# One layer's memory projection moved from the middle of the program to its start, its result kept in DRAM

## The chip, the cores and the metric

The kernel runs on 1 core of one Trainium2 chip. The metric is the device time of one execution in microseconds (us). Engines are named as in the profile: PE is the matmul engine (PEld its weight load), DVE the vector engine, ACT the scalar engine, POOL GpSimd, and SP the engine whose queue issues the DMA transfers.

## What is computed

Two networks run one after the other on x (512 positions x 1024 channels, float32). `first_block` modulates a normalised x by a vector computed from c, projects it, and joins a gated convolution and a four-head recurrence; an FFN follows. `second_block` has two layers with different attentions; each layer also attends to a memory of 256 rows. Cut to what matters here:

```python
# first_block
mod = silu(c) @ w_ada + b_ada                       # 1024 -> 6*1024
sh1, sc1, g1, sh2, sc2, g2 = split(mod, 6)
h = rms_norm(x, norm_mix_g) * (1 + sc1) + sh1
proj = h @ w_in + b_in                              # glu, qk, v, o, gates, merge ...
# second_block
mem_n = rmsnorm(mem, g_mem)                         # mem: 256 x 1024
for i in range(2):
    h = rmsnorm(x, g_mix[i])
    mix, q_mem = mixer(h)                           # i = 0: indexed, i = 1: windowed
    k, v = split(mem_n @ w_mem_kv[i], 2)            # the memory projection, 1024 -> 2*256
    x = x + concat(mix, attend(q_mem, k, v)) @ w_out
    x = x + conv_glu_ffn(rmsnorm(x, g_ffn[i]), ...)
```

The memory projection of layer 1 depends on `mem`, `g_mem` and a weight only, not on x.

## The kernel before

Activations lie with channels on the partitions: eight tiles of 128x512. For float32 accuracy each operand is split into a rounded high part and a remainder, and each product is three matmuls (`mm3`, L370, L371 and L372 in the profile). Weights are streamed by `unit`: a DMA into `st` (L346 to L348), a cast to `wh` on ACT (L349), the remainder `wl` on DVE or POOL (L352). `st`, `wh` and `wl` have four buffers each, so the transfer into the fifth waits until the first has been read. Activations use slots: 24 of "hs", 22 of "big", 12 of "q", 8 of "t". A Tile scheduler fixes each engine's instruction order when the program is built; on the chip every engine then works strictly in that order, and all DMAs are issued by SP in one order.

The start: `setup` loads c, the eight tiles of x, a vector table and constants. `block1` squares and sums x (L448 on ACT, L452 on DVE), sums over channels and broadcasts the reciprocal root (L465, L473, L475, L491, L494), then for each k of eight channel tiles computes two columns of the modulation (`ada`: four transfers of 256 KB, each reduced by DVE at L602), the gain (L609), the modulated norm (`mod_norm`: L625 on DVE, high part L628 on ACT, remainder L629 on DVE) and 18 matmuls (six output tiles, three each) with `w_glu0`. These 144 matmuls are called the first stage here.

The memory projection (`mem_proj`) takes for each k one unit of weights (128x512) and one tile of the memory (128x256, `memT`), squares the tile (L448), splits it with the gain (L364, L365) and runs 12 matmuls of 128x256; after eight k it copies four sums (L1338), forms the reciprocal root, scales (L1345, L1352) and splits keys and values. For layer 1 it stands at the end of `ffn2(0)`, between that layer's last matmuls and `layer_b`; its tail runs inside `layer_b` (`mid1`):

```python
            self.mem_next = self.mem_proj(1)     # ffn2(0), L1246
            self.some(self.mem_next, 8)
...
        def mid1():                              # layer_b, L1731
            hold["bb"] = self.bcast(hold["rc"])
            self.run_all(self.mem_next)
```

Of the kernel before, what the change touches and what calls it, by code (L numbers as in the profile page):

```python
# [4 lines left out]
F32 = mybir.dt.float32  # L5
# [3 lines left out]
ALU = mybir.AluOpType  # L9
# [3 lines left out]
P = 128  # L13
S = 512
D = 1024
KD = D // P
# [6 lines left out]
MEM = 256  # L23
# [76 lines left out]
def _pairs(a, b):  # L100
# [4 lines left out]


_VEC = [
    ("b_ada", 48), ("norm_mix_g", 8), ("b_glu", 16), ("dw_w", 248), ("dw_b", 8),
    ("ln_g", 8), ("ln_b", 8), ("b_pw", 8), ("qkc_w", 64), ("qkc_b", 16), ("b_qk", 16),
    ("b_o", 8), ("b_merge", 16), ("b_if", 1), ("mnorm_g", 8), ("nffn_g", 8), ("fin_g", 8),  # L110
    ("g_mix", 16), ("g_ffn", 16), ("g_mem", 8), ("kv_norm", 2), ("fc_w", 132), ("fc_b", 44),
]
_OFF = {}
_n = 0
# [3 lines left out]
NVEC = _n  # L118
NFIRST = _OFF["b_glu"]
# [107 lines left out]
class Net:  # L227
# [279 lines left out]
    def setup(self):  # L507
        nc = self.nc
        cp = self.cp
        ones = cp.tile([P, P], F32, name="ones")  # L510
        nc.vector.memset(ones, 1.0)
        self.ones = ones
        eps = cp.tile([P, 1], F32, name="eps")
        nc.vector.memset(eps, EPS)
        self.eps = eps
        self.siluc = []
        for i in range(2):
            c = self.t()[0:1, :]
            nc.sync.dma_start(out=c, in_=self.io["c"][:, i * 512:(i + 1) * 512])
            nc.scalar.activation(out=c, in_=c, func=AF.Silu)  # L520
            pt = self.ps()
            nc.tensor.matmul(pt, ones[0:1, :], c, start=True, stop=True)
            self.siluc.append(self.slot("q"))
            nc.scalar.copy(self.siluc[i], pt)

        nc.scalar.activation(out=self.sm(1, "sd")[0:1, :], in_=c[:, 0:1], func=AF.Sqrt, scale=0.0,
                             bias=eps[0:1, :])
        self.x = []
        for k in range(KD):
            x = cp.tile([P, S], F32, name=f"x{k}")  # L530
            self.x.append(x)
            nc.sync.dma_start(out=x, in_=self.io["xT"][k * P:(k + 1) * P, :])
        vec = cp.tile([P, NVEC], F32, name="vec")
        nc.sync.dma_start(out=vec[:, :NFIRST], in_=self.io["vec"][:, :NFIRST])
        self.vec = vec
        cst = cp.tile([P, NCONST], F32, name="cst")
        nc.sync.dma_start(out=cst[:, :P], in_=self.io["const"][:, :P])
        self.cst = cst
        self.ident = cst[:, 0:P]
        self.band = cst[:, P:3 * P]  # L540
        self.inv = {32: cst[:, 3 * P:3 * P + 16], 16: cst[:, 3 * P + 16:3 * P + 24]}
        zeros = cp.tile([P, 2], F32, name="zeros")
        nc.vector.memset(zeros, 0.0)
        self.zeros = zeros
        self.mod = cp.tile([P, 48], F32, name="mod")
        self.aff = cp.tile([P, 16], F32, name="aff")

    def setup_rest(self):
        nc = self.nc
# [660 lines left out]
    def ffn2(self, l):  # L1210
        nc = self.nc
        hold = {}
        h = self.scaled(lambda k: self.v("g_ffn", 8 * l + k))
        acc = self.sumsq(self.x)

        def mid0():
            hold["rc"] = self.rstd(self.colsum(acc), NB, D)

        def mid1():
            hold["bb"] = self.bcast(hold["rc"])  # L1220

        def up(t, pt, act):
            i = t // 2
            if t % 2 == 0:
                a, y = self.t(), self.t()
                nc.vector.tensor_mul(a, pt, hold["bb"])
                w0 = (l * KF + i) * 3
                for step in self.dwconv(y, a, lambda j: self.v("fc_w", w0 + j),
                                        self.v("fc_b", l * KF + i), 3):
                    step()  # L1230
                nc.scalar.activation(out=y, in_=y, func=AF.Silu)
                hold["a"] = y
                return
            b = self.t()
            nc.vector.tensor_mul(b, pt, hold["bb"])  # L1235
            nc.gpsimd.tensor_tensor(out=b, in0=b, in1=hold["a"], op=ALU.mult)  # L1236
            act.append(self.two("big"))
            self.split(act[-1][0], act[-1][1], b)

        def add(n, pt):  # L1240
            nc.vector.tensor_add(self.x[n], pt, self.x[n])

        if l == 0:
            self.groups("f_up0", h, up, lambda f0, n, act: self.tmat("f_down0", f0, n, KD, act, add),
                        (mid0, mid1))
            self.mem_next = self.mem_proj(1)  # L1246
            self.some(self.mem_next, 8)
            return
        ys = []
        ss = [self.sm(2, f"fss{b}", bufs=1) for b in range(NB)]  # L1250
        gf = [self.slot("q"), self.slot("q")]
        for c in range(2):
            nc.sync.dma_start(out=gf[c], in_=self.io["g_fin"][:, c * 512:(c + 1) * 512])

        def turn():
            mid1()
            for b in range(NB):
                for c in range(2):
                    pt = self.ps()
                    for i in range(4):  # L1260
                        self.transpose(pt[:, i * P:(i + 1) * P],
                                       self.x[4 * c + i][:, b * P:(b + 1) * P])
                    ys.append(self.slot("q"))
                    nc.scalar.copy(ys[-1], pt)

        def down(f0, n, act):
            last = f0 + n == KF
            for c in range(2):
                def done(b, pt):
                    y = ys[2 * b + c]  # L1270
                    nc.vector.tensor_add(y, pt, y)
                    if not last:
                        return
                    sq = self.t()
                    nc.scalar.activation(out=sq, in_=y, func=AF.Square, accum_out=ss[b][:, c:c + 1])
                    nc.vector.tensor_mul(y, y, gf[c])
                    if c == 1:
                        t = self.sm(1, "fs1")
                        nc.vector.tensor_add(t, ss[b][:, 0:1], ss[b][:, 1:2])
                        r = self.rstd(t, 1, D, tag="rfin")  # L1280
                        nc.scalar.activation(out=ys[2 * b], in_=ys[2 * b], func=AF.Copy, scale=r)
                        nc.vector.tensor_scalar(out=y, in0=y, scalar1=r, scalar2=None, op0=ALU.mult)
                        for i in range(2):
                            nc.sync.dma_start(
                                out=self.out[0, b * P:(b + 1) * P, i * 512:(i + 1) * 512],
                                in_=ys[2 * b + i])
                self.mmat("f_down1", f0 + c * n // 2, n, act, done, tail=2 if last and c else 0)
        self.groups("f_up1", h, up, down, (mid0, turn))
# [18 lines left out]
        nc.vector.tensor_sub(x[:, :, 0, :], t[0][:, :, 0, :], t[1][:, :, 1, :])  # L1307
        nc.vector.tensor_add(x[:, :, 1, :], t[0][:, :, 1, :], t[1][:, :, 0, :])

    def mem_proj(self, layer):  # L1310

        nc = self.nc
        acc = self.t(MEM)
# [2 lines left out]
        for u in range(KD // 2):  # L1316
            for i in range(2):
                wh, wl = self.unit("w_mem", layer * 4 + u, i)
                k = 2 * u + i
# [4 lines left out]
                hi, lo = both[:, 0:MEM], both[:, MEM:2 * MEM]  # L1324
# [7 lines left out]
                    self.mm3(pv[b], hi[:, r], lo[:, r], wh[:, c], wl[:, c], k == 0, k == KD - 1)  # L1332
                if k < KD - 1:
                    yield
        kv = [self.t(), self.t()]
        kv = [z[:, i * MEM:(i + 1) * MEM] for z in kv for i in range(2)]
        for z, pt in zip(kv, pts):
            nc.scalar.copy(z, pt)  # L1338
        yield
        rc = self.rstd(self.colsum(acc, nb=2), 2, D, tag="rmem")  # L1340
        bc = self.bcast(rc, 2, out=self.t(MEM))
        keys, vals = [], []
        for n in range(2):
            t = self.t(MEM)
            nc.vector.tensor_mul(t, kv[n], bc)  # L1345
            both = self.slot("big", dt=F32R)
            hi, lo = both[:, 0:MEM], both[:, MEM:2 * MEM]
            self.split(hi, lo, t)
            keys.append((hi, lo))
        for b in range(2):  # L1350
            t = self.t(MEM)
            nc.vector.tensor_scalar(out=t, in0=kv[2 + b], scalar1=rc[:, b:b + 1], scalar2=None,  # L1352
                                    op0=ALU.mult)
            vals.append(self.padded(t.rearrange("p (h d) -> p h d", h=4)))
        self.mem = keys, vals

    def padded(self, src, scale=None):

# [360 lines left out]
    def layer_b(self):  # L1719
        nc = self.nc  # L1720
# [9 lines left out]

        def mid1():  # L1731
            hold["bb"] = self.bcast(hold["rc"])
            self.run_all(self.mem_next)

        def done_kv(b, pt):
            rc = hold["rc"][:, b:b + 1]
# [118 lines left out]
    def run(self):  # L1855
        tc = self.tc
        with (tc.tile_pool(name="const", bufs=1) as self.cp,
              tc.tile_pool(name="small", bufs=4) as self.smp,
              tc.tile_pool(name="weights", bufs=3) as self.wp,
              tc.tile_pool(name="slots", bufs=1) as self.sp,  # L1860
              tc.tile_pool(name="psum", bufs=8, space=PSUM) as self.psp):
            self.setup()
            self.block1()
# [24 lines left out]
```

## Time and profile before

| what | value |
|---|---|
| median of 3 runs | 2208.05 us (2207.01 to 2211.64) |
| the profiled execution's own time | 2214.43 us |
| its span (first to last instruction) | 2212.4 us |
| PE busy | 2151.1 us, 97% of the span |
| DVE, ACT, POOL busy | 1470.8, 1036.3, 670.3 us |
| data moved | 217.03 MB, mean 98 GB/s |

Busy time is summed over the whole span; the profiled execution lies 6.4 us above the median, and times inside the program below are those of that one execution. "Granted clock" is the TensorE clock as a share of full speed.

### The profile page before, as it was taken

To read this page: it belongs to the slowest core of one execution; us is meant where nothing else is said; L and a number is where in the kernel's file an instruction comes from. 1 tells how busy PE (TensorE), PEld (TensorE's weight loads), DVE (VectorE), ACT (ScalarE), POOL (GpSimd) and SP (SyncE) were. 2 spreads that over 40 slices of the span, in tenths; PEclk is the share of its full clock that TensorE was granted. 3 is DMA by queue.
4 is the path that set the end of the run, shared out by engine and by line. 5 is a ranking of instruction groups with operands and counts; after the bars stand their busy time and mean duration, and the time that the engine had idled before them with its cause. 6 is when DMAs were issued, how large, how long until landed. Compare 5 with 4: busy or idle time off the path is not lost.

```text
span 2212.4 us, 30653 instructions
## 1 busy us (share of the span) xinstructions
PE 2151.1 (97%) x10708; PEld 1774.0 (80%) x10708; DVE 1470.8 (66%) x2801; ACT 1036.3 (47%) x1953; POOL 670.3 (30%) x606
## 2 busy tenths in 40 slices
PE   6999999999999999998999999999999999999998
PEld 4887778888888989877788888888887878888886
DVE  8889889454876959859975644535546665445354
ACT  3655466654533434644464433423546545324233
POOL 3554454562223626333442110101223321101010
PEclk9999999999999999999999999999999999999999
DMA  7344443233353332321212322332321012223322
GB/s 262 110 135 134 133 133 99 85 96 112 106 163 103 103 102 85 100 72 44 76 48 67 99 92 95 96 96 92 114 90 53 28 54 86 93 94 95 96 94 87
DMA packets 120542, 217.03 MB, mean 98 GB/s; under 512 B 13762, under 2 KB 18114, under 8 KB 120388
## 3 DMA queue, kind: packets, MB, share of 16 engines
q1 hardware_dynamic: 120388, 215.08, 30.7%
q8 instruction: 84, 1.38, 0.2%
q14 instruction: 70, 0.57, 0.1%
HBM read 212.93 MB, written 2.10 MB: 97 GB/s over the span
## 4 chain that ended last, share of the span: by engine, by line
PE 77%; DVE 5%; issue 1%; ACT 1%; POOL 1%; DMA 0%; SPq 0%; ACTq 0%; POOLq 0%; DVEq 0%
PE ps L370 25%; PE ps L371 25%; PE ps L372 25%; PE ps L504 2%; DVE bias L1634 1%; DVE m L1633 1%; DVE bias L1596 0%; DVE x L1510 0%; DVE rope L1305 0%; PE ps L465 0%; DMA q<-in_ada_dram 0%; POOL q L1096 0%; PE ps L494 0%; DVE pt L362 0%; POOL wl L1096 0%
## 5 line engine op out<-in xcount | busy, mean ns | idle before, releaser
L349 ACT CAST wh<-st 128x512 fp32r<-128x512 f32 (+1 forms) x634 | 388.0, 616 | 689.9 <-PE ps L371 429.8
L371 PE MATMUL ps<-hs,wh 128*128 128x512 f32 (+1 forms) x1736 | 662.0, 381 | 4.1 <-DVE hs L629 3.9
L370 PE MATMUL ps<-hs,wh 128*128 128x512 f32 (+1 forms) x1736 | 658.8, 383 | 7.0 <-ACT hs L1001 2.5
L372 PE MATMUL ps<-hs,wl 128*128 128x512 f32 (+1 forms) x1736 | 659.7, 381 | 1.7 <-POOL wl L1096 1.7
L352 DVE TENSOR_TENSOR wl<-st,wh 128x512 fp32r<-128x512 f32 x424 | 307.9, 728 | 206.5 <-ACT wh L349 204.6
L352 POOL TENSOR_TENSOR wl<-st,wh 128x512 fp32r<-128x512 f32 (+1 forms) x210 | 287.5, 1376 | 352.0 <-ACT wh L349 328.8
L370 PEld LDWEIGHTS ps<-hs,wh 128*128 128x128 f32 x1736 | 327.0, 189 | 79.8 <-ACT hs L628 4.7
L371 PEld LDWEIGHTS ps<-hs,wh 128*128 128x128 f32 x1736 | 327.7, 189 | 73.9 <-DVE hs L629 6.5
L372 PEld LDWEIGHTS ps<-hs,wl 128*128 128x128 f32 x1736 | 327.4, 189 | 70.4 <-POOL wl L1096 2.1
L1236 POOL TENSOR_TENSOR t<-t,t 128x512 f32<-128x512 f32 x44 | 69.0, 1569 | 603.0 <-DVE t L1235 533.9
L644 DVE SCALAR_TENSOR_TENSOR big<-ps,vec,big 128x511 f32<-128x511 f32 (+28 forms) x240 | 164.7, 718 | 3.5 <-ACT big L641 3.5
L372 PE MATMUL ps<-big,wl 128*128 128x512 f32 x400 | 156.3, 394 | 2.8 <-DVE wl L352 2.8
L371 PE MATMUL ps<-big,wh 128*128 128x512 f32 x400 | 156.9, 394 | 0.0
L370 PE MATMUL ps<-big,wh 128*128 128x512 f32 x400 | 156.3, 394 | 0.0
L370 PE MATMUL ps<-wh,hs 128*128 128x512 f32 (+1 forms) x320 | 124.3, 394 | 2.9 <-ACT t L952 2.9
L362 DVE TENSOR_TENSOR big<-t,big 128x512 fp32r<-128x512 f32 (+1 forms) x102 | 72.6, 728 | 80.9 <-ACT big L361 80.5
L371 PE MATMUL ps<-wl,hs 128*128 128x512 f32 (+1 forms) x320 | 125.0, 391 | 0.0
L372 PE MATMUL ps<-wh,hs 128*128 128x512 f32 (+1 forms) x320 | 124.6, 389 | 0.0
L452 POOL TENSOR_TENSOR t<-t,t 128x512 f32<-128x512 f32 (+1 forms) x51 | 65.5, 1285 | 173.3 <-ACT t L448 171.6
L361 ACT CAST big<-t 128x512 fp32r<-128x512 f32 (+1 forms) x102 | 52.9, 535 | 105.3 <-POOL t L1236 83.6
L372 PEld LDWEIGHTS ps<-big,wl 128*128 128x128 f32 x400 | 75.1, 188 | 21.2 <-DVE wl L352 3.7
L370 PEld LDWEIGHTS ps<-big,wh 128*128 128x128 f32 x400 | 75.1, 188 | 17.7
(396 smaller groups left out, 3769.8 us busy)
## 6 DMA issues: line engine op xcount, KB each, us to landing
st<-in_f_up_dram SPq DMA_DIRECT2D x176, 256.0 KB, 2.6
st<-in_f_down_dram SPq DMA_DIRECT2D x88, 256.0 KB, 2.6
st<-in_w_up_dram SPq DMA_DIRECT2D x56, 256.0 KB, 2.7
st<-in_ada_dram SPq DMA_DIRECT2D x48, 256.0 KB, 2.7
st<-in_w_down_dram SPq DMA_DIRECT2D x44, 256.0 KB, 2.6
big<-in_ada_dram SPq DMA_DIRECT2D x32, 256.0 KB, 5.1
st<-in_w_qk_dram SPq DMA_DIRECT2D x32, 256.0 KB, 2.7
st<-in_w_ogm_dram SPq DMA_DIRECT2D x32, 256.0 KB, 2.6
```

The costliest lines, as they stand in the source:

```text
L349: nc.scalar.copy(wh, st)
L352: eng.tensor_tensor(out=wl, in0=st, in1=wh.bitcast(F32), op=ALU.subtract)
L361: nc.scalar.copy(hi, src)
L362: nc.vector.tensor_sub(lo, src, hi.bitcast(F32))
L370: nc.tensor.matmul(out, lh, rh, start=start, stop=False)
L371: nc.tensor.matmul(out, lh, rl, start=False, stop=False)
L372: nc.tensor.matmul(out, ll, rh, start=False, stop=stop)
L452: (add or nc.gpsimd).tensor_tensor(out=acc, in0=acc, in1=sq, op=ALU.add)
L504: self.nc.tensor.transpose(out, in_, self.ident[:p, :p])
L644: nc.vector.scalar_tensor_tensor(out=out[:, d:], in0=x[:, :S - d], scalar=w(j), in1=out[:, d:], op0=ALU.mult, op1=ALU.add)
L1236: nc.gpsimd.tensor_tensor(out=b, in0=b, in1=hold["a"], op=ALU.mult)
L1633: nc.vector.max(m8, sc)
```

## The change

The projection of layer 1 is built in `setup`, before x is loaded. `mem_proj` is cut into `mem_sums` (up to the scaled sums) and `mem_split` (the split). `mem_keep` runs `mem_sums(1)` and writes the two result tiles (128x512 each) to a DRAM tile `kept`; `mem_load` reads them back in `layer_b` and splits them. `g_mem` moves into the part of the vector table that is loaded first, this load comes first, and the weight remainders go to POOL from here on (`pool_lo`).

```diff
@@ _VEC
-    ("b_ada", 48), ("norm_mix_g", 8), ("b_glu", 16), ...
+    ("b_ada", 48), ("norm_mix_g", 8), ("g_mem", 8), ("b_glu", 16), ...
@@ setup
+        vec = cp.tile([P, NVEC], F32, name="vec")
+        nc.sync.dma_start(out=vec[:, :NFIRST], in_=self.io["vec"][:, :NFIRST])
+        self.vec = vec
         self.siluc = []
...
-        self.x = []
-        for k in range(KD):
-            x = cp.tile([P, S], F32, name=f"x{k}")
-            self.x.append(x)
-            nc.sync.dma_start(out=x, in_=self.io["xT"][k * P:(k + 1) * P, :])
-        vec = cp.tile([P, NVEC], F32, name="vec")
-        nc.sync.dma_start(out=vec[:, :NFIRST], in_=self.io["vec"][:, :NFIRST])
-        self.vec = vec
...
+        self.pool_lo = 1
+        mem = self.mem_keep()
+        self.some(mem, 4)
+        self.x = []
+        for k in range(KD):
+            x = cp.tile([P, S], F32, name=f"x{k}")
+            self.x.append(x)
+            nc.sync.dma_start(out=x, in_=self.io["xT"][k * P:(k + 1) * P, :])
+        self.run_all(mem)
@@ ffn2
-            self.mem_next = self.mem_proj(1)
-            self.some(self.mem_next, 8)
             return
@@ mem_sums (the end of what was mem_proj)
-        kv = [self.t(), self.t()]
-        kv = [z[:, i * MEM:(i + 1) * MEM] for z in kv for i in range(2)]
+        two = [self.t(), self.t()]
+        kv = [z[:, i * MEM:(i + 1) * MEM] for z in two for i in range(2)]
...
+    def mem_keep(self):
+        _, two = yield from self.mem_sums(1)
+        self.kept = self.dp.tile([P, 2 * S], F32, name="kept")
+        for i in range(2):
+            self.nc.sync.dma_start(out=self.kept[:, i * S:(i + 1) * S], in_=two[i])
+
+    def mem_load(self):
+        two = [self.t(), self.t()]
+        for i in range(2):
+            self.nc.sync.dma_start(out=two[i], in_=self.kept[:, i * S:(i + 1) * S])
+        self.mem_split([z[:, i * MEM:(i + 1) * MEM] for z in two for i in range(2)])
@@ layer_b
         def mid1():
             hold["bb"] = self.bcast(hold["rc"])
-            self.run_all(self.mem_next)
+            self.mem_load()
```

Lines move with the change: what was L602, L625, L628, L629 of `block1` is L607, L630, L633, L634 in the rows of the changed kernel.

The scheduler's order at the start, first on SP, which issues the transfers. Before, these are the rows where the loads of x end and those of the modulation (`in_ada_dram`) begin:

```order
L532 DMA x_102<-in_xT_dram 128x512
L532 DMA x_104<-in_xT_dram 128x512
L534 DMA vec<-in_vec_dram 128x56
L537 DMA cst<-in_const_dram 128x128
L600 DMA big_156<-in_ada_dram 128x512
L600 DMA big_160<-in_ada_dram 128x512
```

With the change, SP's rows 59 to 68 at the end of all 32 modulation loads; `memT` k=4 to k=7 are the tiles q_229, q_255, q_281 and q_307:

```order
L605 DMA big_761<-in_ada_dram 128x512
L605 DMA big_765<-in_ada_dram 128x512
L561 DMA posi<-in_pos_dram 128x4
L1747 DMA sk_15823<-in_sinks_dram 128x16
L348 DMA st_469<-in_w_glu_dram 128x384
L1324 DMA q_229<-in_memT_dram 128x256
L1324 DMA q_255<-in_memT_dram 128x256
L348 DMA st_484<-in_w_glu_dram 128x384
L1324 DMA q_281<-in_memT_dram 128x256
L1324 DMA q_307<-in_memT_dram 128x256
```

Half of the memory's tiles stand behind the last modulation load, and the last two also behind the load into st_484, whose buffer is that of the last `w_mem` unit.

On DVE, before, the start of the program after the memsets (L452 sums the squares of x, L602 reduces a modulation load):

```order
L452 TENSOR_TENSOR t_114<-t_114,t_131 128x512
L602 ISA big_156,ada_158<-big_156,q_79,vec 128x512
L602 ISA ada_158 128x1
L452 TENSOR_TENSOR t_114<-t_114,t_134 128x512
L602 ISA big_160,mod<-big_160,q_86,ada_158 128x512
```

With the change, DVE's rows 79 to 90 (the 32nd modulation load is big_765; L365 is the remainder of a memory tile; rmem is the memory's reciprocal root; t_353 is the sum of the squares of x):

```order
L607 ISA big_765,mod<-big_765,q_90,ada_763 128x512
L607 ISA mod 128x1
L614 SCALAR_TENSOR_TENSOR aff<-mod,vec 128x1
L365 SCALAR_TENSOR_TENSOR q_234<-q_229,vec,q_234 128x256
L365 SCALAR_TENSOR_TENSOR q_260<-q_255,vec,q_260 128x256
L365 SCALAR_TENSOR_TENSOR q_286<-q_281,vec,q_286 128x256
L365 SCALAR_TENSOR_TENSOR q_312<-q_307,vec,q_312 128x256
L475 RECIPROCAL rmem_338<-sd_336 128x2
L491 TENSOR_TENSOR t_342<-cst,rmem_338 128x256
L1348 TENSOR_SCALAR t_328<-t_328,rmem_338 128x256 x2
L1346 TENSOR_TENSOR t_327<-t_327,t_340 128x256 x2
L452 TENSOR_TENSOR t_353<-t_353,t_355 128x512
```

The seven additions for x, which stood ahead of the reductions, now stand behind all 32 of them and behind the memory projection's end; behind them follow eight L630 in a row, then the L634. ACT's order has the squares of x behind the copy of the memory's broadcast in the same way. On PE all 96 matmuls of the projection stand ahead of x's column sums and of the whole first stage.

On PE between the two layers, before (ps_15507 is the last sum of the FFN, q_15547 a memory tile; 96 rows of 128x256 begin here):

```order
L371 MATMUL ps_15507<-big_15298,wh_15515 128x512
L372 MATMUL ps_15507<-big_15297,wl_15516 128x512
L370 MATMUL ps_15534<-q_15547,wh_15539 128x256
L371 MATMUL ps_15534<-q_15547,wh_15539 128x256
L372 MATMUL ps_15534<-q_15547,wl_15540 128x256
```

With the change, the same place (ps_15742 is the last sum of the FFN, hs_15768 the first tile of the next layer's input):

```order
L371 MATMUL ps_15742<-big_15533,wh_15750 128x512
L372 MATMUL ps_15742<-big_15532,wl_15751 128x512
L370 MATMUL ps_15825<-wh_15830,hs_15768 128x512
L371 MATMUL ps_15825<-wl_15831,hs_15768 128x512
```

The 96 matmuls are gone from here. The two reads of `kept` stand in SP's order right behind the column sums of layer 1's input, and their first use on DVE about 60 matmuls later.

## Rows read from the trace of the kernel before

**Rows 1.** The page's busy time of each engine.
```profile
PE 2151.1 (97%) x10708; PEld 1774.0 (80%) x10708; DVE 1470.8 (66%) x2801; ACT 1036.3 (47%) x1953; POOL 670.3 (30%) x606
```

**Rows 2.** Busy times by stretch; the last three columns: granted clock, DMA share, GB/s.
```profile
0.00:10.00 10.00, 3.77 (x4) 1.16 (x4) 2.70 (x7) 8.24 (x14) 0.70 (x6) 1.00 0.70 240
10.00:35.00 25.00, 16.39 (x52) 11.18 (x52) 24.59 (x50) 7.41 (x15) 9.64 (x8) 1.00 1.04 379
35.00:40.00 5.00, 4.46 (x13) 3.51 (x14) 5.00 (x15) 0.72 (x1) 0.00 (x0) 0.66 0.92 314
0.00:61.00 61.00, 42.65 (x141) 29.23 (x142) 49.00 (x102) 23.64 (x42) 21.16 (x23) 0.97 0.72 250
150.00:350.00 200.00, 191.61 (x869) 155.21 (x869) 186.27 (x364) 102.83 (x166) 98.90 (x78) 0.98 0.42 131
```

**Rows 3.** Timeline of ACT at the start: start, duration, instruction, count, idle time before.
```profile
8.90 2.40 ACT L448 ACTIVATE t<-x 128x512 f32<-128x512 f32 x4
14.16 1.02 ACT L349 CAST wh<-st 128x384 fp32r<-128x384 f32 x2 [2.86 <-DMA st<-in_w_glu_dram]
15.18 0.26 ACT L473 ACTIVATE sd<-ps,eps 128x4 f32<-128x4 f32 x1
```

**Rows 4.** The memory tiles' transfers, from issue to landing.
```profile
DMA to landing us min/median/max: 2.0/2.5/3.8
```

**Rows 5.** Timeline of ACT around the projection of layer 1.
```profile
1554.89 0.49 ACT L364 ACTIVATE q<-q,vec 128x256 fp32r<-128x256 f32 x1
...
1595.65 0.92 ACT L1338 COPY t<-ps 128x256 f32<-128x256 f32 x3
...
1621.96 0.37 ACT L499 COPY t<-ps 128x256 f32<-128x256 f32 x1 [0.20 <-PE ps L494]
```

**Rows 6.** Timeline of PE around the projection of layer 1.
```profile
1584.85 0.28 PE L370 MATMUL ps<-q,wh 128*128 128x256 f32 x1
...
1596.36 0.40 PE L370 MATMUL ps<-wh,hs 128*128 128x512 f32 x1
...
1619.43 0.55 PE L465 MATMUL ps<-ones,t 128*128 128x64 f32 x4
...
1620.35 0.39 PE L372 MATMUL ps<-wh,hs 128*128 128x512 f32 x1
...
1621.52 0.58 PE L370 MATMUL ps<-wh,hs 128*128 128x512 f32 x1
```

**Rows 7.** Timeline of DVE at the start.
```profile
9.56 2.28 DVE L452 TENSOR_TENSOR t<-t,t 128x512 f32<-128x512 f32 x3 [0.31 <-ACT t L448]
...
46.52 1.50 DVE L602 CUSTOM_DVE_ANT_0 big<-big,q,ada 128x512 f32<-128x512 f32 x1
...
48.02 0.74 DVE L602 CUSTOM_DVE_ANT_0 big<-big,q,vec 128x512 f32<-128x512 f32 x1
...
53.59 0.74 DVE L625 SCALAR_TENSOR_TENSOR t<-x,aff,ps 128x512 f32<-128x512 f32 x1
54.25 0.31 DVE L609 SCALAR_TENSOR_TENSOR aff<-mod,vec 128x1 f32<-128x1 f32 x1
```

**Rows 8.** Timeline of PE in the first stage, and the next stage's first matmul.
```profile
13.17 1.97 PE L465 MATMUL ps<-ones,t 128*128 128x64 f32 x8 [6.60 <-DVE t L452]
17.73 2.08 PE L494 MATMUL ps<-t,ones 128*128 128x512 f32 x2 [2.59 <-DVE t L491]
...
38.50 0.63 PE L372 MATMUL ps<-hs,wl 128*128 128x512 f32 x1
...
42.27 0.40 PE L371 MATMUL ps<-hs,wh 128*128 128x512 f32 x1
...
44.37 0.39 PE L372 MATMUL ps<-hs,wl 128*128 128x512 f32 x1
...
60.83 0.39 PE L370 MATMUL ps<-hs,wh 128*128 128x512 f32 x1
```

**Rows 9.** Timeline of POOL in the first stage.
```profile
42.21 5.25 POOL L352 TENSOR_TENSOR wl<-st,wh 128x384 fp32r<-128x384 f32 x4 [7.28 <-ACT wh L349]
```

More of the change, by code (lines that the diff above doesn't have):

```diff
@@ L107 @@
 _VEC = [
-    ("b_ada", 48), ("norm_mix_g", 8), ("b_glu", 16), ("dw_w", 248), ("dw_b", 8),
+    ("b_ada", 48), ("norm_mix_g", 8), ("g_mem", 8), ("b_glu", 16), ("dw_w", 248), ("dw_b", 8),
     ("ln_g", 8), ("ln_b", 8), ("b_pw", 8), ("qkc_w", 64), ("qkc_b", 16), ("b_qk", 16),
     ("b_o", 8), ("b_merge", 16), ("b_if", 1), ("mnorm_g", 8), ("nffn_g", 8), ("fin_g", 8),
-    ("g_mix", 16), ("g_ffn", 16), ("g_mem", 8), ("kv_norm", 2), ("fc_w", 132), ("fc_b", 44),
+    ("g_mix", 16), ("g_ffn", 16), ("kv_norm", 2), ("fc_w", 132), ("fc_b", 44),
 ]
@@ L1308, in do_rope, with mem_sums @@
         nc.vector.tensor_add(x[:, :, 1, :], t[0][:, :, 1, :], t[1][:, :, 0, :])
-    def mem_proj(self, layer):
+    def mem_sums(self, layer):
         nc = self.nc
@@ L1341, in mem_proj, with mem_split @@
         bc = self.bcast(rc, 2, out=self.t(MEM))
+        for n in range(2):
+            nc.vector.tensor_mul(kv[n], kv[n], bc)
+        for b in range(2):
+            nc.vector.tensor_scalar(out=kv[2 + b], in0=kv[2 + b], scalar1=rc[:, b:b + 1],
+                                    scalar2=None, op0=ALU.mult)
+        return kv, two
+    def mem_split(self, kv):
         keys, vals = [], []
         for n in range(2):
-            t = self.t(MEM)
-            nc.vector.tensor_mul(t, kv[n], bc)
             both = self.slot("big", dt=F32R)
             hi, lo = both[:, 0:MEM], both[:, MEM:2 * MEM]
-            self.split(hi, lo, t)
+            self.split(hi, lo, kv[n])
             keys.append((hi, lo))
         for b in range(2):
[L1351 to L1354, printed above, removed]
+            vals.append(self.padded(kv[2 + b].rearrange("p (h d) -> p h d", h=4)))
         self.mem = keys, vals
+    def mem_proj(self, layer):
+        kv, _ = yield from self.mem_sums(layer)
+        self.mem_split(kv)
+    def mem_keep(self):
[8 more added lines that the diff above has]
+        self.mem_split([z[:, i * MEM:(i + 1) * MEM] for z in two for i in range(2)])
     def padded(self, src, scale=None):
@@ L1860, in run @@
               tc.tile_pool(name="slots", bufs=1) as self.sp,
+              tc.tile_pool(name="kept", bufs=1, space=bass.MemoryType.DRAM) as self.dp,
               tc.tile_pool(name="psum", bufs=8, space=PSUM) as self.psp):
```

## The prediction

> **What bounds the kernel now.** The page's busy times come first [rows 1]: PE is busy 97% of the span, so inside the program a microsecond of matmuls taken away or a microsecond of PE idleness added is a microsecond of time, unless PE would have waited there anyway. Then the table of stretches, to see where PE does wait [rows 2]: in the first 61 us it is busy 42.65 us and idle 18.35, the largest gap; from 150 to 350 us it waits 200 - 191.61 = 8.4 us. What fills the gap at the start? The DMA share in the same rows: 1.04 of the engines at 379 GB/s between 10 and 35 us, with DVE busy 24.59 of those 25 us. So PE idles at the start because data arrives at a limit and DVE works them off at nearly the same pace. A projection moved there does not meet an idle machine; it meets an idle PE behind a full DMA queue and a full DVE. What counts is therefore the order in which SP, DVE, ACT and PE take the work at the start, since none of them overtakes. The timelines of the start [rows 3, 7, 8] and of the old place [rows 5, 6] give the durations.
>
> **What the change removes.** In the old place PE runs the 96 matmuls from 1584.85 to 1596.36 without a gap: 11.51 us [rows 6]. The tail in layer 1 goes too: the two column sums' four matmuls, 0.55, and from the end of a matmul (1620.35 plus its slot of 0.23) to 1621.52 the broadcast with its wait, 0.94. Together **-13.0 us**, on PE, which is full there. Nothing should take their place: the first input tiles of layer 1 are ready, and the one finished last is first used 84 matmuls later (84 x 0.233 = 19.6 us; the spacing is worked out below). The two reads of `kept` are 256 KB each, land some 2.5 us after issue like the memory's tiles [rows 4], and are used about 60 matmuls (14 us) later. I cost them at nothing; without that cover they would cost up to 2.5 us. The two writes stand behind loads that are needed much later: nothing.
>
> **What it does to the start, step by step.**
> 1. *The transfers.* Up to the last modulation half, SP's new order has 60 transfers: 8 units of `w_mem` (2.10 MB), x (2.10), four memory tiles (0.52), 32 modulation halves (8.39), two `w_glu0` units (0.39), vector table, constants and c (0.58): 14.08 MB. Before, the first 10 us moved 10 x 0.240 = 2.40 MB, then 379 GB/s [rows 2]. So the last half is there at 10 + 11.68/0.379 = 40.8 us. How long after its arrival by rate is data used? Before, 3.44 MB stand up to the first `w_glu0` unit, 12.8 us by rate, and its cast started at 14.16 [rows 3]: 1.4 us. DVE has the last half at 42.2 and is done at about 43.
> 2. *The last two memory tiles.* They stand behind the load into st_484, which waits until POOL has read the last `w_mem` unit. That unit's cast needs the buffer that the k=3 matmuls read, and the k=3 memory tile is the 54th transfer, some 4 us before the last half. Its square, split, matmuls, the cast and POOL's remainder take till about 44. From there issue to landing 2.5 [rows 4] and two issues: the last tile is usable at **47.5**.
> 3. *The projection's end.* ACT's square and high part 2 x 0.49 [rows 5] = 0.9; DVE's remainder 0.4 (half the width of a 0.74 [rows 7]); the last 12 matmuls at 11.51/96 = 0.12 each, 1.4; four copies at 0.31, 1.2; a cast that stands behind them on ACT, 0.5 [rows 3]; then from the column sums to the end of the broadcast's copy, 1619.43 to 1621.96 + 0.37 [rows 5, 6], 2.9. The copy ends at **54.8**.
> 4. *The squares of x* stand behind that copy on ACT: 0.60 each [rows 3], and the seven additions at 0.76 on DVE [rows 7]. First addition after two squares, 1.2; then 5.3: **61.3**. Before, this was over at 13.1, since x came first and the additions stood ahead of the reductions.
> 5. *Root and broadcast:* 1.97 + 0.26 + 0.74 + 2.08 [rows 3, 7, 8] and 0.3 for the reciprocal and hand-overs, an estimate: 5.4. **66.7**.
> 6. *Norm:* eight L630 stand in a row ahead of the first remainder. Two neighbours start 0.66 apart (53.59, 54.25 [rows 7]), so 8 x 0.67 + 0.74 = 6.1: **72.8**. Until then PE can run only six of the stage's 144 matmuls.
> 7. *The stage:* 138 matmuls. Nine lie between 42.27 and 44.37 [rows 8]: 0.233 each, 32.2 us. After idling PE ran slower for a while: from 35 to 40 us the granted clock was 0.66, between the full 2.4 GHz and the lower level of 1.2, and a matmul took 0.63 instead of 0.40 [rows 2, 8]. Some nine such matmuls at 0.2 more: 1.8. Later weights keep up: two casts and two remainders of 1.3 on POOL [rows 9] per 18 matmuls (4.2 us). End at **106.8**.
>
> Before, the next stage began at 60.83 [rows 8]. The start is therefore 46.0 us later. From there PE is almost always busy, so I pass the shift on in full.
>
> **Sum:** +46.0 - 13.0 = **+33.0 us**. Against the profiled execution's own 2214.43 that is 2247.4; it lies 6.4 above the median, and the same difference on the median 2208.05 gives **2241 us**.
>
> **A rule weighed against the trace.** While POOL computes remainders (42.21 to 47.46 [rows 9]), a reduction on DVE that otherwise takes 0.74 takes 1.50 [rows 7]. In the changed order four remainders of `w_mem` and three additions on POOL fall among the reductions. If each stretches one, that is 7 x 0.76 = 5.3 us, and the k=3 remainder on which step 2 rests stands among those reductions. I count nothing, since DVE has waits for data to give in this stretch, and keep 5.3 for the upper end. The Trainium skill, "SBUF — State Buffer", section "Who interferes with whom", says that a DVE instruction with two SBUF inputs contends with a GpSimd instruction that reads SBUF; the trace agrees with 1.50 against 0.74. By that rule, taken to the full, the sum would be 2246 rather than 2241.
>
> **Rivals.**
> - *The projection is hidden in PE's 18.35 idle us* [rows 2], and all that is left is the gain: 2208 - 13 = 2195, faster. For it: 11.5 us of matmuls fit into 18.35 by size. Against it: x's column sums stand behind all 96 matmuls on PE, and their squares behind the memory's tail on ACT. It decides at the place of the squares of x: were the sum of x finished before about 20 us, when the modulation needs it, this would hold. Chance 0.06, for an order on the chip that differs from the one I read.
> - *Only the transfers count:* 3.15 MB more at the start (`w_mem`, memory, early parts) at 379 GB/s is 8.3 us, less 13.0: 2203, a gain of about 0.2%. It needs x's norm to be done early as well, only paced by the later modulation. Chance 0.04, about same.
> - *The shift is partly swallowed.* From 150 to 350 us PE waits 8.4 us [rows 2], for DVE, whose convolution work begins with the first stage's outputs. If those waits have causes that don't shift (transfers long done), up to 8.4 come back: 2233. Against it: DVE is busy 186.27 of these 200 us with work that starts later by the same shift. It is inside the range; 0.12.
> - *POOL and DVE hold each other up* as weighed above: 2246, 0.15, inside the range.
>
> **How the numbers follow.** The likeliest case, the step-by-step sum with full pass-through, has 0.63, and the two variants inside the range 0.27. Downwards the range takes swallowed waits (-8.4), a faster chain of the last memory tile (-2), no slow-clock stretch (-1.8), a little faster transfers (3% on step 1 would be -0.9): not all at once, 2226. Upwards contention (+5.3), an exposed read of `kept` (+2.5), more time on the slow clock (+2) and what the scheduler rearranges elsewhere (a few us): 2256. A measurement of this kernel tells about 0.2%, 4.4 us. Slower by more than that: 0.90; within it: 0.04; faster: 0.06.
>
> **What the new profile would show.** Step 1: DMA share near 1 to about 41 us, and DVE's last reduction at about 43. Steps 2 and 3: the last `memT` landing near 47, PE's matmuls of 128x256 ending near 50 with gaps between the k, the memory's broadcast copied near 55. Step 4: eight squares of x in a row on ACT only after that. Step 6: PE's first L370 of 128x512 near 68, steady from 73. Step 7: the first stage's end near 107, with a granted clock under 1 in some stretch between 55 and 80. Old place: the FFN's last L372 followed at once by an L370 of 128x512, and no wait for the split of `kept`. The prediction is wrong if x's column sums run before 30 us, if PE waits in layer 1 for the read tiles, or if the 46 us shrink after the first stage, which the start of each later stage against the old trace would show.

## The result, and the profile after

The changed kernel takes 2243.39 us (median of 4 runs, 2241.49 to 2244.77); the kernel before, in the runs beside it, 2209.85 us (2207.01 to 2212.03). The ratio is 1.0151, 95% interval [1.0136, 1.0165]: **33.5 us slower**, where 33.0 were forecast (2241, range 2226 to 2256).

The profiled execution of the change has a span of 2239.5 us (its own time 2241.49). The table of stretches at its start, with the columns of [rows 2]:

```profile
0.00:10.00 10.00, 3.78 (x4) 1.16 (x4) 0.18 (x3) 7.22 (x11) 4.50 (x10) 1.00 0.68 211
10.00:35.00 25.00, 9.23 (x36) 8.05 (x36) 17.35 (x45) 4.30 (x9) 7.03 (x6) 1.00 1.05 389
35.00:40.00 5.00, 1.28 (x6) 1.28 (x6) 4.93 (x14) 0.82 (x2) 0.73 (x1) 1.00 1.06 387
...
40.00:55.00 15.00, 10.22 (x57) 9.34 (x57) 10.10 (x25) 5.39 (x14) 7.44 (x8) 1.00 0.34 99
55.00:75.00 20.00, 7.81 (x24) 4.82 (x22) 12.12 (x22) 9.57 (x21) 1.39 (x2) 0.59 0.17 56
```

The queue is full until 40 us, as step 1 had it; PE does 1.28 us of work between 35 and 40 and 7.81 between 55 and 75, where before it was in the first stage and, from 65 us on, in the next one. The timeline of ACT shows the forecast chain:

```profile
37.85 0.42 ACT L448 ACTIVATE t<-q 128x256 f32<-128x256 f32 x1 [6.46 <-DMA q<-in_memT_dram]
...
48.95 0.42 ACT L448 ACTIVATE t<-q 128x256 f32<-128x256 f32 x1 [2.90 <-DMA q<-in_memT_dram]
...
50.61 0.41 ACT L448 ACTIVATE t<-q 128x256 f32<-128x256 f32 x1
...
58.51 0.37 ACT L499 COPY t<-ps 128x256 f32<-128x256 f32 x1 [2.03 <-PE ps L494]
58.78 4.27 ACT L448 ACTIVATE t<-x 128x512 f32<-128x512 f32 x8
```

The fourth memory tile is squared at 37.85, the eighth at 50.61, the memory's broadcast is copied until 58.88, and only then do the eight squares of x follow, in a row. DVE's timeline:

```profile
31.82 1.63 DVE L607 CUSTOM_DVE_ANT_0 big<-big,q,ada 128x512 f32<-128x512 f32 x1
...
41.75 0.48 DVE L365 SCALAR_TENSOR_TENSOR q<-q,vec,q 128x256 fp32r<-128x256 f32 x1
...
46.11 1.29 DVE L607 CUSTOM_DVE_ANT_0 big<-big,q,ada 128x512 f32<-128x512 f32 x1
...
59.96 5.47 DVE L452 TENSOR_TENSOR t<-t,t 128x512 f32<-128x512 f32 x7 [0.29 <-ACT t L448]
...
70.93 5.36 DVE L630 SCALAR_TENSOR_TENSOR t<-x,aff,ps 128x512 f32<-128x512 f32 x8 [2.17 <-PE ps L494]
76.20 5.38 DVE L634 SCALAR_TENSOR_TENSOR hs<-t,mod,hs 128x512 fp32r<-128x512 f32 x8
107.77 0.75 DVE L687 SCALAR_TENSOR_TENSOR hs<-ps,vec,t 128x512 f32<-128x512 f32 x1 [26.18 <-ACT t L685]
```

Between 20 and 45 us DVE is busy 24.65 of 25 us. It reaches the remainder of the memory's k=4 tile only behind its last reduction, and PE waits for that remainder:

```profile
47.92 0.87 DVE L365 SCALAR_TENSOR_TENSOR q<-q,vec,q 128x256 fp32r<-128x256 f32 x2
...
48.45 0.58 PE L371 MATMUL ps<-q,wh 128*128 128x256 f32 x1 [1.40 <-DVE q L365]
...
55.00 0.56 PE L465 MATMUL ps<-ones,t 128*128 128x64 f32 x4
```

From 48.45 PE runs the projection's last 42 matmuls in a row until the column sums at 55.00.

The sums of x end at 65.43; before, the additions ended at 13.1 [rows 7 show three of them]. The eight L630 stand in one block ahead of the first L634. The last line is DVE's first use of a finished output of the first stage, called the *first output* below. In the first trace of the kernel before, the same instruction is L682:

```profile
63.50 0.75 DVE L682 SCALAR_TENSOR_TENSOR hs<-ps,vec,t 128x512 f32<-128x512 f32 x1 [6.61 <-ACT t L680]
```

So the start is 44.3 us later. The end of the first stage has moved as far, and it lies elsewhere than the prediction puts it. Its first matmul before is at 21.40; of the stage's 144 matmuls only 126 start ahead of 60.83 [rows 8], so that row is the first of the stage's last 18 matmuls and not yet the next stage's first. These rows count PE's matmuls from 21.30 on; then come the first matmuls of the next stage, before and with the change:

```profile
21.30:60.80 39.50, 34.63 (x126) 25.62 (x127) 35.35 (x73) 11.57 (x22) 16.96 (x14) 0.96 0.63 218
21.30:65.00 43.70, 38.83 (x144) 29.00 (x145) 36.51 (x75) 15.71 (x28) 19.84 (x16) 0.96 0.61 211
...
65.03 0.39 PE L370 MATMUL ps<-hs,wh 128*128 128x512 f32 x1
...
109.30 0.40 PE L370 MATMUL ps<-hs,wh 128*128 128x512 f32 x1
```

PE's timeline, at the start and at the old place of the projection:

```profile
72.48 2.93 PE L370 MATMUL ps<-hs,wh 128*128 128x512 f32 x6 [1.59 <-ACT hs L633]
77.00 0.50 PE L371 MATMUL ps<-hs,wh 128*128 128x512 f32 x1 [1.59 <-DVE hs L634]
...
1624.70 0.40 PE L372 MATMUL ps<-big,wl 128*128 128x512 f32 x1
1624.93 0.39 PE L370 MATMUL ps<-wh,hs 128*128 128x512 f32 x1
...
1645.54 1.02 PE L494 MATMUL ps<-t,ones 128*128 128x512 f32 x2
```

The FFN's last matmul is followed at once by layer 1. The place that was at 1584.85 before [rows 6] is at 1624.93, 40.1 us later; the same L370 of layer 1 that began at 1596.36 comes 28.6 later, and behind the tail the distance is 27.1, which is also the difference of the spans (2239.5 - 2212.4): the old place gives back 13.0 us in these two traces. That 27.1 is less than the 33.5 of the medians is explained below: the first trace of before is a long one.

### The profile page after: what moved, and what is told of

It reads as the page before. It is cut to its first block, busy times and chain, and to the rows that moved or that the text cites. A ratio compares the mean times of both kernels' runs of the same rounds, so it can differ in the third digit from the quotient of the medians.

```text
span 2239.5 us, 30666 instructions
## 1 busy us (share of the span) xinstructions
PE 2155.8 (96%) x10708; PEld 1779.4 (79%) x10708; DVE 1464.9 (65%) x2793; ACT 1037.0 (46%) x1953; POOL 674.9 (30%) x614
## 4 chain that ended last, share of the span: by engine, by line
PE 74%; DVE 5%; issue 2%; ACT 1%; POOL 1%; DMA 0%; SPq 0%; POOLq 0%; ACTq 0%; DVEq 0%
PE ps L370 24%; PE ps L371 24%; PE ps L372 24%; PE ps L504 2%; DVE bias L1657 1%; DVE m L1656 1%; DVE bias L1619 0%; DVE x L1533 0%; POOL q L1101 0%; POOL t L1165 0%; PE ps L465 0%; DVE rope L1308 0%; DMA q<-in_w_up_dram 0%; POOL wl L1101 0%; PE ps L494 0%
## 5 line engine op out<-in xcount | busy, mean ns | idle before, releaser
L370 PE MATMUL ps<-hs,wh 128*128 128x512 f32 (+1 forms) x1736 | 660.6, 383 | 7.1 <-ACT hs L1006 2.5
L352 DVE TENSOR_TENSOR wl<-st,wh 128x512 fp32r<-128x512 f32 x416 | 301.0, 726 | 200.6 <-ACT wh L349 199.2
L352 POOL TENSOR_TENSOR wl<-st,wh 128x512 fp32r<-128x512 f32 (+1 forms) x218 | 296.2, 1365 | 391.4 <-ACT wh L349 377.8
L370 PEld LDWEIGHTS ps<-hs,wh 128*128 128x128 f32 x1736 | 326.6, 189 | 79.5 <-ACT hs L1006 3.4
L370 PE MATMUL ps<-big,wh 128*128 128x512 f32 x400 | 156.4, 394 | 0.0
L370 PE MATMUL ps<-wh,hs 128*128 128x512 f32 (+1 forms) x320 | 125.8, 398 | 3.2 <-ACT t L957 3.2
L452 POOL TENSOR_TENSOR t<-t,t 128x512 f32<-128x512 f32 (+1 forms) x51 | 64.7, 1269 | 171.4 <-ACT t L448 170.8
L361 ACT CAST big<-t 128x512 fp32r<-128x512 f32 (+1 forms) x102 | 52.7, 535 | 109.3 <-POOL t L1241 85.5
L370 PEld LDWEIGHTS ps<-big,wh 128*128 128x128 f32 x400 | 75.1, 188 | 17.6
```

The source lines that it names most:

```text
L352: eng.tensor_tensor(out=wl, in0=st, in1=wh.bitcast(F32), op=ALU.subtract)
L361: nc.scalar.copy(hi, src)
L370: nc.tensor.matmul(out, lh, rh, start=start, stop=False)
L452: (add or nc.gpsimd).tensor_tensor(out=acc, in0=acc, in1=sq, op=ALU.add)
```

## The experiments

Each kernel is the changed one with one thing done otherwise; the expectation is quoted from before the run. "First output" is read from DVE's timeline (63.5 before, 107.8 with the change).

**No projection at all.** The kept tiles are filled with a constant, x is loaded first.

```diff
-        mem = self.mem_keep(); self.some(mem, 4); ... ; self.run_all(mem)
+        self.mem_keep()                       # x loaded before it
 def mem_keep(self):
-        _, two = yield from self.mem_sums(1)
+        two = [self.t(), self.t()]
+        for z in two:
+            self.nc.vector.memset(z, 0.01)
```

> Leaves out the projection of layer 1: its kept tiles are filled with a constant at the start, and layer 1 reads and splits them as in the change; x is loaded first, as before. Theory (the order at the start costs some 46 us, the old place gives back 13): nothing at the start, so only the gain is left, 13.0 us below before, about 2197 (2193 to 2200), DVE's first output of the first stage at 63.5 us as before. Rival (the two reads of kept make layer 1 wait): 2199 or more, with an idle PE in front of their use. Rival (the gain is swallowed): near 2210.

Measured 2197.21 us against 2210.09 beside it, ratio 0.9941 [0.9926, 0.9955]: 12.9 us less, where the sum had 13.0. First output at 66.06. Against the first trace of before the matmuls ahead of layer 1 are 3.2 us early, and those behind its tail 16.5: 13.3 given back. So the term for the old place is right, and the reads of `kept` take nothing back.

**The bytes alone.** As above, but the 3.15 MB are loaded between x and the modulation and not used.

```diff
+        for k in range(KD):
+            d = self.slot("big"); nc.sync.dma_start(out=d, in_=...w_mem unit k of layer 1)
+        for k in range(KD):
+            d = self.slot("big", MEM); nc.sync.dma_start(out=d, in_=...memT tile k)
         self.mem_keep()
```

> As the kernel without the projection, but the 3.15 MB of weights and memory tiles are loaded at the start, between x and the modulation, and not used. Theory (order): the bytes shift the start by 3 to 8 us at most (3.15 MB at 379 GB/s is 8.3, and DVE had loads in hand for part of it), so 2200 to 2205. Rival (the bytes in the queue are what makes the change slow): a start that is 40 us or more later, 2237 or more. Rival (bytes are hidden behind DVE's backlog): as without them, 2197.

Measured 2205.19 us, ratio 0.9975 [0.9964, 0.9986]; first output at 74.59, 8.5 later than without the loads, and 8.0 us more by the medians. The bytes cost what 3.15 MB at 379 GB/s come to (8.3 us), and not 46. "Only the transfers count" is thereby a kernel of its own: were that all, the change would take 2205.

**x first.** x's loads, squares, sums, root and broadcast ahead of the projection; memory tiles as in the change.

```diff
         bc = self.bcast(self.rstd(self.colsum(self.sumsq(self.x, ...)), NB, D), out="psum")
+        self.run_all(self.mem_keep())         # here, instead of in setup
```

> The change, but x is loaded, summed and its root broadcast before the projection; the projection's matmuls still stand ahead of the first stage and its last four memory tiles still behind the modulation loads. Theory: steps 4 to 6 (squares, sums, root) leave the path, the memory chain of steps 1 to 3 stays: the first stage starts near 58 instead of 72, its first output on DVE near 92 to 95 instead of 107.8, total 2226 (2219 to 2232). Rival (the place of x alone makes the change slow): first output within 10 us of 63.5, total near 2205. Rival (the place of x costs nothing, the memory tiles all): 2243, as the change.

Measured 2234.83 us, ratio 1.0109 [1.0093, 1.0124]; first output at 95.67, forecast 92 to 95. The start is 12.1 us earlier than with the change, the total only 8.6 by the medians (forecast 17). The start moved nearly as forecast, but the total lies 9 us above the forecast and outside its range. PE's timeline shows what bounds it now:

```profile
42.08 0.58 PE L371 MATMUL ps<-q,wh 128*128 128x256 f32 x1 [3.41 <-DVE q L365]
...
45.21 0.79 PE L370 MATMUL ps<-q,wh 128*128 128x256 f32 x2 [1.48 <-ACT q L364]
...
50.03 0.58 PE L371 MATMUL ps<-q,wh 128*128 128x256 f32 x1 [3.18 <-DVE q L365]
...
59.75 0.70 PE L494 MATMUL ps<-t,ones 128*128 128x256 f32 x2 [2.17 <-DVE t L491]
...
61.69 2.93 PE L370 MATMUL ps<-hs,wh 128*128 128x512 f32 x6 [1.24 <-ACT hs L630]
```

The memory's matmuls wait for their tiles' splits, and the first stage comes at once behind the memory's broadcast.

**Memory tiles first.** All eight are loaded ahead of weights, x and modulation.

```diff
         pk, pv = pts[0:2], pts[2:4]
+        raws = [self.slot("big", MEM) for _ in range(KD)]
+        for k, raw in enumerate(raws):
+            nc.sync.dma_start(out=raw, in_=self.io["memT"][k * P:(k + 1) * P, :])
```

> The change, but all eight memory tiles are loaded first, ahead of weights, x and modulation. Theory: the memory chain ends near 30 us instead of 55; the sums of x now lie between the reductions, but its eight L630 stand behind all 32 of them, so the first stage starts near 50 and runs 138 matmuls in a row: first output on DVE near 86 to 90 instead of 107.8, total 2221 (2214 to 2229). Rival (the memory tiles' place costs nothing, only that of x does): 2243, as the change. Rival (the memory tiles' place is all): near 2200.

Measured 2232.01 us, ratio 1.0096 [1.0074, 1.0118]; first output at 96.35, later than the forecast 86 to 90, and the total 11 us above the forecast and outside its range. The memory's broadcast indeed ran at 30 us, but x did not follow as early as I had put it:

```profile
30.22 0.70 PE L494 MATMUL ps<-t,ones 128*128 128x256 f32 x2 [0.71 <-DVE t L491]
...
49.66 1.97 PE L465 MATMUL ps<-ones,t 128*128 128x64 f32 x8 [18.75 <-DVE t L452]
...
55.18 2.07 PE L494 MATMUL ps<-t,ones 128*128 128x512 f32 x2 [3.55 <-DVE t L491]
...
58.85 2.92 PE L370 MATMUL ps<-hs,wh 128*128 128x512 f32 x6 [1.59 <-ACT hs L633]
```

PE waits 18.75 us for the sums of x, whose seven additions the scheduler strewed among the reductions, and another 3.55 for the broadcast's diagonal, which stands there too. Each of the two orders holds the start up by itself.

**Both first.** x's chain first and all memory tiles right behind x.

```diff
         bc = self.bcast(self.rstd(self.colsum(self.sumsq(self.x, ...)), NB, D), out="psum")
+        self.run_all(self.mem_keep())         # with the eight loads at its head
```

> The change, but x is loaded, summed and its root broadcast first, and all eight memory tiles are loaded right behind x. Theory (order, then bytes): both chains leave the path, the 96 matmuls fall into PE's idle time, and what remains are the bytes, measured with 8 us in the kernel that only loads, and some 5 us of extra DVE work (eight L365 of 0.4, the scaling); first output on DVE at 75 to 80 us, total 2208 (2203 to 2213). Rival (the projection's work on PE costs its 11.5 us at the start in any order): first output at 86 or later, 2215 to 2222. Rival (an early place costs as much in any order): 2230 or more.

Measured 2215.27 us, ratio 1.0030 [1.0017, 1.0042]; first output at 81.62. With both orders mended 26.2 of the 44.3 us go; what is left over the kernel that only loads (74.59) is 7.0 us, for the projection's work. Which engine makes it up is not shown: DVE's last reduction starts 3.6 us later than in the kernel that only loads (65.40 against 61.84), and up to the first output PE is busy 13.4 us more and idle 6.4 us less. Forecast were 75 to 80 and 2208; both were missed, and the total lies in the range of the rival that lets PE pay for its matmuls (2215 to 2222), while the first output does not (86 or later). So PE's idle time hid about half of its extra work. The kernel is better than the change by 28 us, but not better than before, since 18 us at the start are paid for 13 given back.

**Behind the first stage.** `mem_keep` runs after the first stage; x and modulation as before.

```diff
         for n in range(FIRST):
             glu_done(n, pts[n])
+        self.run_all(self.mem_keep())
```

> The same projection with its result kept in DRAM, but built behind the first stage instead of ahead of it, with x and the modulation as before. Theory (the place at the start costs, not the early computation or the way through DRAM): PE pays its 11.5 us in a busy place, less what it would have waited there for DVE, and layer 1 gives back 13.2: 2206 (2200 to 2211). Rival (the way through DRAM or holding the work early costs by itself): 2215 or more.

Measured 2221.33 us, ratio 1.0053 [1.0033, 1.0072]: 10 us above the upper end of the forecast (2206, at most 2211) and where the rival put it. But it is not the way through DRAM, as the rival has it: that cost nothing in the kernel without projection. PE's timeline:

```profile
82.33 1.12 PE L465 MATMUL ps<-ones,t 128*128 128x64 f32 x4 [5.87 <-POOL t L452]
...
84.52 1.22 PE L494 MATMUL ps<-t,ones 128*128 128x256 f32 x2 [1.08 <-DVE t L491]
```

The memory's column sums stand on PE ahead of the next stage's matmuls and wait 5.87 us for POOL, which has the additions of squares queued between weight remainders of the next stage; the wait is followed by a stretch at a granted clock of 0.74 to 0.75:

```profile
65.00:75.00 10.00, 10.00 (x86) 10.00 (x85) 2.95 (x5) 7.71 (x19) 9.53 (x10) 1.00 0.56 167
75.00:85.00 10.00, 3.05 (x18) 2.66 (x17) 1.12 (x6) 5.52 (x12) 7.27 (x8) 0.75 0.47 138
85.00:95.00 10.00, 10.00 (x34) 7.95 (x34) 9.96 (x32) 3.72 (x7) 2.34 (x2) 0.74 0.34 106
```

Between 75 and 85 PE works 3.05 of 10 us, and about ten of its matmuls behind the wait take 0.63 us instead of 0.40. My expectation priced the 96 matmuls and left out the tail, a chain over POOL, PE, ACT and DVE that stands in the queues.

**In layer 0, where PE waits.** `mem_keep` ahead of layer 0's memory attention.

```diff
+        self.run_all(self.mem_keep())
         mo = self.weave(self.mem_attn(qm), self.take(q0, 8), 0.7)
```

> The same projection with its result kept in DRAM, but built in layer 0 right ahead of its memory attention, where PE waited 3.75 us for a split of ACT and later 2.83 us. Theory (what counts is whether PE waits at the place): 11.5 us of matmuls less the 3.75 waited, the tail of about 1 us, less 13.2: 2204 (2200 to 2208). Rival (PE waits in another place instead, as it needs the same work of ACT and DVE): 2209 to 2213. Rival (both waits are filled): 2201.

Measured 2217.12 us, ratio 1.0028 [1.0016, 1.0039]; forecast 2204, wrong. Against the first trace of before, the shift goes from 0.1 us ahead of the place to 19.4 behind it, instead of the 8 to 9 expected. In the stretch table of this kernel DVE is busy all the time, and PE does 2.63 us of work in the 10 us ahead of the projection:

```profile
1015.00:1025.00 10.00, 2.63 (x16) 1.62 (x16) 10.00 (x21) 4.34 (x10) 1.97 (x2) 0.87 0.27 79
1025.00:1035.00 10.00, 8.85 (x49) 8.55 (x49) 10.00 (x29) 5.67 (x15) 7.21 (x8) 0.61 0.21 67
1035.00:1045.00 10.00, 6.47 (x53) 6.13 (x51) 10.00 (x32) 5.28 (x13) 9.54 (x9) 0.90 0.54 160
```

PE's longest wait there, 7.37 us, ends with ACT's split of the first memory tile at 1024.66. Read along the queues, it goes back to DVE's selection of keys: the tile's load stands on SP behind a load of weights that was issued at 1020.27; this one needed a buffer that POOL's remainder had read until 1020.25; and the remainder stood behind a mask of the selection, for which POOL waited 7.89 us for DVE (L1617). The projection also hangs on the same DVE for its remainders and its tail (PE waited 4.02 us for the broadcast's diagonal), so its matmuls do not fill the wait, they lengthen it.

**Beside layer 0's projection.** `mem_keep` at the start of the first FFN, its eight steps behind the broadcast there, its tail in the FFN's own `mid`.

```diff
         bc = self.bcast(rc, out="psum")
+        mem1 = self.mem_keep()
+        self.some(mem1, 8)
...
         def mid():
             self.run_all(mem)
+            self.run_all(mem1)
```

> The same projection with its result kept in DRAM, but built at the start of the first FFN, right behind the projection of layer 0, where PE waited 0.60 us for a broadcast and 2.55 us for the first split input. Theory (a place pays only as far as PE waits there and the tail lies beside other work): 11.5 us less the 3.15 waited, the tail beside the FFN's first matmuls, less 13.2: 2206 (2203 to 2209). Rival (as in the place of layer 0's attention, ACT and DVE fall behind and the FFN's first inputs come later): 2212 to 2220.

Measured 2212.79 us, ratio 1.0011 [0.9999, 1.0022]: no difference from before that can be told. The waits of 0.60 and 2.55 us did not pay: from 538 to 568 us PE is idle 3.43 us, where before it was 3.15. From 558 to 568 ACT and DVE are both busy 10.00 of 10 us, and PE's waits end with DVE (1.61 and 0.68 us) and ACT (1.04). No place was found in which the projection is cheaper than in its own.

**Both kernels once more,** unchanged, for a second trace each.

> The kernel before, unchanged, for a second trace. Its first trace lay some 4 us above the median of its runs. Theory (the shift at the start is passed on in full, and the 4 us lost between 100 and 1550 us in the comparison are the spread between executions): this trace differs from the first by several us in the first block and by none in layer 1. Rival (PE's waits in the first block swallow a part of any shift): this trace agrees with the first within 1 us throughout.

> The changed kernel unchanged, for a second trace, to see what of the comparison repeats. Theory: the first stage's first output on DVE at 107.8 us and the 13.2 us given back between 1550 and 1650 us repeat within 0.5 us, and any difference between the two traces lies between 100 and 650 us. Rival (the start itself varies by several us): the first output differs by over 2 us.

Before: 2206.87 us, span 2204.9; first output at 61.28. Laid beside the first trace, equal instructions are 2.2 us early at the start, 6.7 at 400 us, 7.1 to 7.6 from 700 us on, and 7.5 to the end, layer 1 included. The difference lies wholly in the first 650 us. The change: 2249.23 us; its first output is late, against my expectation, and the 13.0 us between the last matmul ahead of layer 1 and the end repeat:

```profile
112.33 0.75 DVE L687 SCALAR_TENSOR_TENSOR hs<-ps,vec,t 128x512 f32<-128x512 f32 x1 [28.97 <-ACT t L685]
```

4.6 us of its 7.7 longer span arise in the start. The stretches of this second trace:

```profile
10.00:35.00 25.00, 9.30 (x36) 8.05 (x36) 16.53 (x40) 4.47 (x10) 6.73 (x6) 0.84 1.04 383
35.00:55.00 20.00, 10.35 (x46) 9.47 (x47) 16.16 (x43) 5.41 (x13) 7.25 (x8) 0.52 0.53 181
55.00:75.00 20.00, 7.80 (x34) 5.40 (x34) 10.36 (x19) 8.60 (x20) 2.50 (x3) 0.65 0.19 57
75.00:90.00 15.00, 13.41 (x42) 10.07 (x41) 8.35 (x13) 5.86 (x10) 5.01 (x4) 0.67 0.10 27
```

The granted clock was 0.84, 0.52, 0.65 and 0.67 here, where the first trace had 1.00 up to 55 us, 0.59 to 75 and 0.98 to 90. Not all of the 4.6 us go with that. 1.1 are there already at the first reduction (18.71 instead of 17.65), up to which both traces have 1.00. The memory's last matmuls add 0.6: they took 0.41 us each until 54.0 and then 0.28, in the first trace until 51.6. The first 18 matmuls behind the first remainder add 2.8: most took 0.63 us instead of 0.40.

The traces were not all taken on one chip. The spread is not the chips' alone, though: 19 executions of the kernel before on one chip lie between 2204.58 and 2215.95 us.

## Why the prediction was right, step by step

The forecast was 33.0 us, +46.0 at the start and -13.0 in the old place; the medians give 33.5. What makes the kernel slow, the two orders at the start, and what the old place gives back were read rightly. That the sum is within 0.5 us is luck: the end of the old stage was misread, 4.2 us too early, and 1.8 us were put for a slow clock that cost nothing in the first trace, which together made up for a memory chain that ended 4.1 us later than reckoned; and two executions of one kernel differ by several us. With the old stage's end at 65.0 the prediction's own steps give 41.8 at the start and +28.8 in all, 2237 us. By the traces:

- *Step 1, the transfers:* 389 GB/s to 35 us against the 379 reckoned; the queue is full to 40 us, as said, and the last modulation half, issued at 36.8, landed 5.9 us later at 42.7 (42.2). But DVE began its reduction only at 46.11 and ended it at 47.4 instead of 43: from 20 us on DVE, and not the data, set the pace, which the step had the other way round. It was held up by POOL and by a cast of positions (1.23 us instead of 0.16). That counted, for the k=4 tile's remainder stands behind this reduction.
- *Step 2, the last memory tile:* it landed at 50.0 instead of 47.5. The k=3 tile's remainder stood in DVE's order until 41.75, 3.1 us after ACT's part was done, and the load of st_484 waited for POOL until 46.2 instead of 44. Nor was this tile what ended last: it was split by 52.07, but PE, in arrears since its wait for the k=4 tile, took it up at 53.55. These two, 2.5 and 1.5 us, make the term some 4 us too small.
- *Steps 3 to 6* carried that on: copy at 58.9 (54.8), sums of x at 65.4 (61.3), first L630 at 70.9 (66.7), steady matmuls from 77.0 (72.8). From the squares on, each step took as long as reckoned within 0.1 us.
- *Step 7, the stage:* its steady part began 4.2 us later than reckoned and ended 2.5 later, at 109.3 (106.8): no slow clock cost anything there in the first trace, and the 138 matmuls ran in 32.3 us, 0.40 us each. In the second trace of the change the slow stretch is there, with 2.8 us where 1.8 were put. The step's other end was misread: before, the stage ended at 65.03 and not at 60.83. So the shift is 44.3 us, not 46.0, at the stage's end and at the first output alike; against the second trace of before it is 46.5.
- *The shift is passed on:* between the first traces 4.2 us of it are lost before layer 1 (44.3 to 40.1). Against the second trace of before, 46.5 at the start become 47.8 ahead of layer 1: nothing is swallowed. The rival of swallowed waits rested on a stretch whose waits change by 4 us between two executions of one kernel, and one pair of traces cannot tell it from that spread. The nine traces that differ at the start and in the old place alone can together: from the first output to the last matmul ahead of layer 1 they take 1515 to 1523 us, with first outputs from 61 to 112 us, and the late ones (1517 and 1520 with the change) do not take less than the early ones (1521 and 1516 before). So 8.4 us are not taken back; a us or two may be.
- *The old place:* -13.0 between the first traces and 13.3 in the kernel without projection. The reads of `kept` landed in some 3.5 us instead of 2.5, and ACT waited 1.1 us for them, so the 14 us of cover that I had counted were not there; PE did not wait, so the price of nothing stands though its reason does not.
- *The rule that was weighed:* reductions of 1.63 and 1.29 instead of 0.74 stand where POOL works. The Trainium skill, "SBUF — State Buffer", section "Who interferes with whom", has it so, and the trace agrees with 1.63. The price of nothing was wrong, and so was its reason, for DVE had no waits to give. Seven of the 32 reductions, each begun while POOL worked, took 0.95 to 1.70 us, together 3.65 us more than at 0.745 each, of the 5.3 kept for the upper end. 3.1 of the 3.65 stand ahead of the k=3 remainder and so went into step 2.
- *The rivals:* "hidden in PE's idle time" and "only the transfers" are excluded by the squares of x at 58.8 and by the kernel that only loads (8 us). The kernels in between share the start's cost out, by first outputs: 8.5 us for the bytes, 7.0 for the projection's work, and 26.2 for the two orders, x behind the projection and the memory tiles behind the modulation, of which mending one alone brings 12.1 or 11.4. From no projection (66.06) these steps are 66.06 + 8.5 + 7.0 + 26.2 = 107.8, by construction. Each is read from single traces whose start varies by 2 to 5 us; by the medians, each against the kernel before beside it, they are 8.0, 9.7 and 28.8.

What stays open: whether the first block takes back a us or two of any shift, why the spread of several us lies there, and which engine the projection's 7 to 10 us at the start go to.

## What to carry to other kernels

An idle PE is no free place: what counts is whether the work's own chain (transfers, splits, sums, tail) finds room on the engines that PE waits for, and here three places with PE waits (start, layer 0's attention, FFN start) all cost as much as or more than the busy place. When work is put ahead of other work, read the order on every queue and look for the chain that now stands behind it; both the x chain and the memory tiles cost more than the bytes and the matmuls. Price a moved stage with its serial tail, not by its matmuls alone. And count the matmuls up to the row that is taken for a stage's end: the next stage's rows can look the same.

## What the runs showed of the hardware

Two executions of the same program differ by 7.5 us in span (2212.4 and 2204.9), all of it in the first 650 us, after which equal instructions keep their distance within about 1 us. And the clock in a stretch with an idling PE is not the same in each execution: 1.00 and 0.52 of full speed (2.4 GHz, and little over the lower level of 1.2) were granted to the same 35 to 55 us of one program. That record does not tell the pace of the matmuls there: from 47 to 51 us those of 128x256 took 0.41 us each, one every 0.21, in both executions, and only later 0.28, one every 0.12. Of the 4.6 us by which the second execution's first output is later, 3.4 are matmuls at the slow pace.

In the first trace of the change a reduction on DVE that began while an instruction ran on POOL took 0.95 to 1.70 us (seven cases). One that was already running when POOL began kept its 0.75, as at 22.00, 26.67, 31.03, 37.78 and 44.28 us.
